# Combining expert outputs: a ring of nine slots in chunks of three tokens, one token of each chunk summed by TensorE

## The chip, the cores and the metric

The kernel runs on one core of one Trainium2 chip. The metric is the device time of one execution in microseconds; lower is better. The kernel before takes 707.68 us (median of three runs, 707.18 to 707.82). The profile is of one execution of 707.67 us; its span, in which the engines' records lie, is 705.5 us.

## The reference

```python
# expert_outputs: (16, 1024, 8, 512) float32; combine_weights: (16, 1024, 8) float32
def reference(expert_outputs, combine_weights):
    weights = combine_weights[..., np.newaxis]
    return np.sum(expert_outputs * weights, axis=2).astype(np.float32)
```

For each of 16,384 tokens, eight rows of 512 numbers are scaled by eight weights and added. A token brings in 16 KB and gives out 2 KB; all in all 268.4 MB of expert outputs and 0.5 MB of weights are read and 33.6 MB are written. Each number that is read is used in one multiplication and one addition.

## The kernel before

The tokens are spread over the 128 partitions, so a "token" below means one token of each partition: 128 token positions in all, each of them 2.097 MB of input and 0.262 MB of output. 120 of them go through a loop (`LOOP`), the last 8 through a tail (`TAIL`).

**The ring.** `ring` holds R = 10 tokens. A round fills it in three chunks of 4, 4 and 2 tokens (`CHUNKS`, L101), each one DMA with its own semaphore `loaded[c]`. There are 12 rounds. Each partition reads runs that lie together in memory: one partition's stretch is M = 40 tokens (640 KB), so this is the distance between the rows of one DMA.

**The engines.** Each engine has its own program, written out in order, and they meet at semaphores only.

- SyncE (`loads_and_last_stores`) issues all loads. From the second round on, a chunk's load waits until VectorE has finished the tokens that lay in those slots (L99, semaphore `done`, which counts finished tokens). After the loop it issues eight loads of one token each for the tail (L111), then the last round's store and the tail's stores in four pieces (L115).
- ScalarE (`weights_and_stores`) copies each round's weights from `w_t` into `w_c` (L136, two halves in turn) and issues the stores of the other rounds from `acc` (L91), each once its ten tokens are done. After the loop it makes the diagonal matrices for TensorE (L143): `ident` times one weight, 128x128, with five buffers in turn.
- VectorE (`terms`) does all sums of the loop. Per chunk one product of the first expert's rows by a broadcast weight (L189), then seven fused multiply-and-adds per token (L179), two tokens in turn. In the tail it adds the experts that TensorE leaves over.
- TensorE (`first_terms`) works in the tail alone. A product of a diagonal matrix of one weight and the 128x512 rows of one expert scales these rows; several of them accumulate in PSUM (`ps`). `pe_e` says how many experts of each tail token go this way: 43 products in all (L155).
- GpSimd makes the identity matrix at the start.

In the tail the tokens come in one by one, TensorE works on each as it lands, VectorE finishes it, and the stores go out as tokens become ready, the last one for a single token.

Of the kernel before, what the change touches and what calls it, by code (L numbers as in the profile page):

```python
# [10 lines left out]
def kernel(  # L11
# [17 lines left out]

    nc = tc.nc  # L30
    fp32 = mybir.dt.float32
    mult, add = mybir.AluOpType.mult, mybir.AluOpType.add

    B, S, E, D = expert_outputs.shape
    T = B * S
    P = 128
    R = 10
    G = 2 * R
    M = 2 * G
    T_P = T // P  # L40
    GROUPS = T_P // G
    LOOP = GROUPS * G
    TAIL = T_P - LOOP
    ROUNDS = LOOP // R
    CHUNKS = [(0, 4), (4, 4), (8, 2)]
    C = len(CHUNKS)
    DIAGS = 5

    x = expert_outputs.rearrange("b s e d -> (b s) e d")
    w = combine_weights.rearrange("b s e -> (b s) e")  # L50
    o = out.rearrange("b s d -> (b s) d")
    cut = LOOP * P
    x_g = x[0:cut].rearrange("(n p b g) e d -> n b p g e d", p=P, b=2, g=G)
    w_g = w[0:cut].rearrange("(n p m) e -> p n m e", p=P, m=M)
    o_g = o[0:cut].rearrange("(n p b g) d -> n b p g d", p=P, b=2, g=G)
    x_t = x[cut:T].rearrange("(p j) e d -> p j e d", j=TAIL)
    w_x = w[cut:T].rearrange("(p j) e -> p j e", j=TAIL)
    o_t = o[cut:T].rearrange("(p j) d -> p j d", j=TAIL)


    pe_e = [6, 6, 6, 6, 5, 5, 5, 4]
    tail_stores = [(0, 4), (4, 2), (6, 1), (7, 1)]
    diags = [(j, e) for j in range(TAIL) for e in range(pe_e[j])]
# [4 lines left out]
    acc = one.tile([P, G, D], fp32, name="acc")  # L68
    w_t = one.tile([P, T_P, E], fp32, name="w_t")
    w_c = one.tile([P, G, E], fp32, name="w_c")  # L70
    ident = one.tile([P, P], fp32, name="ident")
    diag = one.tile([P, DIAGS, P], fp32, name="diag")
    ps = psum.tile([P, TAIL, D], fp32, name="ps")

    sem = tc.alloc_semaphore
    w_in = sem("w_in")
    w_set = [sem(f"w_set{h}") for h in range(2)]
    loaded = [sem(f"loaded{c}") for c in range(C)]
    stored = [sem(f"stored{h}") for h in range(2)]
    step = sem("step")  # L80
    done = sem("done")
    tail_in = [sem(f"tail_in{j}") for j in range(TAIL)]
    tail_out = sem("tail_out")
    id_set = sem("id_set")
    diag_set = sem("diag_set")
    product = sem("product")

    def store(queue, n):
        h = n % 2
        queue.wait_ge(done, (n + 1) * R)  # L90
        queue.dma_start(  # L91
            out=o_g[n // 4, n // 2 % 2, :, h * R : h * R + R], in_=acc[:, h * R : h * R + R]
        ).then_inc(stored[h], 16)

    def loads_and_last_stores(sync):
        for n in range(ROUNDS):
            for c, (r, m) in enumerate(CHUNKS):
                if n:
                    sync.wait_ge(done, (n - 1) * R + r + m)  # L99
                g = n % 2 * R + r  # L100
                sync.dma_start(  # L101
                    out=ring[:, r : r + m], in_=x_g[n // 4, n // 2 % 2, :, g : g + m]
                ).then_inc(loaded[c], 16)
                if n == 0 and c == 0:
                    sync.dma_start(
                        out=w_t[:, 0:LOOP].rearrange("p (n m) e -> p n m e", m=M), in_=w_g
                    ).then_inc(w_in, 16)
                    sync.dma_start(out=w_t[:, LOOP:T_P], in_=w_x).then_inc(w_in, 16)
        for j in range(TAIL):
            sync.wait_ge(done, LOOP - R + j + 1)  # L110
            sync.dma_start(out=ring[:, j], in_=x_t[:, j]).then_inc(tail_in[j], 16)  # L111
        store(sync, ROUNDS - 1)
        for j, m in tail_stores:
            sync.wait_ge(done, LOOP + j + m)
            sync.dma_start(out=o_t[:, j : j + m], in_=acc[:, j : j + m]).then_inc(tail_out, 16)  # L115
# [13 lines left out]
    def weights_and_stores(scalar):  # L129
        scalar.wait_ge(w_in, 32)  # L130
        for n in range(ROUNDS):
            h = n % 2
            if n >= 2:
                store(scalar, n - 2)
                scalar.wait_ge(stored[h], 16 * (n // 2))
            scalar.copy(  # L136
                out=w_c[:, h * R : h * R + R], in_=w_t[:, n * R : n * R + R]
            ).then_inc(w_set[h], 1)
        store(scalar, ROUNDS - 2)
        scalar.wait_ge(stored[0], 16 * ROUNDS // 2)  # L140
        scalar.wait_ge(id_set, 2)
        for k, (j, e) in enumerate(diags):
            i = scalar.mul(out=diag[:, k % DIAGS], in_=ident, mul=w_t[:, LOOP + j, e : e + 1])  # L143
            i.then_inc(diag_set, 1)
            if k >= DIAGS:
                i.wait_op(product, k - DIAGS + 1, "sem-ge")
        scalar.wait_ge(stored[1], 16 * ROUNDS // 2)
        scalar.wait_ge(tail_out, 16 * len(tail_stores))

    def first_terms(tensor):  # L150
        for k, (j, e) in enumerate(diags):
            if e == 0:
                tensor.wait_ge(tail_in[j], 16)
            tensor.wait_ge(diag_set, k + 1)
            tensor.matmul(  # L155
                ps[:, j],
                lhsT=diag[:, k % DIAGS],
                rhs=ring[:, j, e],
                start=e == 0,
                stop=e == pe_e[j] - 1,  # L160
            ).then_inc(product, 1)

    def terms(vector):
        def take(s, v):
            vector.wait_ge(s, v).then_inc(s, -v)  # L165

        last = {}

        def count(i, g, e):

            if e == E - 1:
                i.then_inc(done, 1)
            else:
                i.then_inc(step, 1)
                last["all"] = last.get("all", 0) + 1
                last[g] = last["all"]

        def fused(g, e, weight, before):
            return vector.scalar_tensor_tensor(  # L179
                out=acc[:, g], in0=ring[:, g % R, e], scalar=weight, in1=before, op0=mult, op1=add  # L180
            )

        with nc.Fori(0, GROUPS, engines=OrderedEngineSet([vector.engine])):
            for h in range(2):
                take(w_set[h], 1)
                for c, (r, m) in enumerate(CHUNKS):
                    take(loaded[c], 16)
                    q = h * R + r
                    i = vector.tensor_tensor(  # L189
                        out=acc[:, q : q + m],  # L190
                        in0=ring[:, r : r + m, 0],
                        in1=w_c[:, q : q + m, 0:1].to_broadcast([P, m, D]),
                        op=mult,
                    )
                    i.then_inc(step, 1)
                    last["all"] = last.get("all", 0) + 1
                    last.update((g, last["all"]) for g in range(q, q + m))
                    for g in range(q, q + m, 2):
                        for e in range(1, E):
                            for k in (g, g + 1):  # L200
                                i = fused(k, e, w_c[:, k, e : e + 1], acc[:, k])
                                i.wait_op(step, last[k], "sem-ge")
                                count(i, k, e)
            take(step, last["all"])

        last.clear()
        for q in ((0, 1), (2,), (3,), (4,), (5,), (6,)):
            for e in range(pe_e[q[0]], E):
                for j in q:
                    weight = w_t[:, LOOP + j, e : e + 1]  # L210
                    if e == pe_e[j]:
                        i = fused(j, e, weight, ps[:, j])
                        i.wait_op(product, sum(pe_e[: j + 1]), "sem-ge")
                    else:
                        i = fused(j, e, weight, acc[:, j])
                        i.wait_op(step, last[j], "sem-ge")
                    count(i, j, e)

        j = TAIL - 1
        for e in range(pe_e[j], E):  # L220
            weight = w_t[:, LOOP + j, e : e + 1]
            if e == pe_e[j]:
                i = vector.tensor_scalar_mul(out=acc[:, j], in0=ring[:, j, e], scalar1=weight)  # L223
                i.wait_op(tail_in[j], 16, "sem-ge")
            else:
                i = fused(j, e, weight, acc[:, j])
                i.wait_op(step, last[j], "sem-ge")
            count(i, j, -1)
        vector.wait_ge(step, last[j])  # L229
        i = vector.tensor_tensor(out=acc[:, j], in0=acc[:, j], in1=ps[:, j], op=add)  # L230
        i.wait_op(product, len(diags), "sem-ge")
        count(i, j, E - 1)

    with tc.tile_critical(no_gpsimd_drain=True):  # L234
        loads_and_last_stores(nc.sync)
        identity(nc.gpsimd)
        weights_and_stores(nc.scalar)
        first_terms(nc.tensor)
        terms(nc.vector)
# [30 lines left out]
```

## Time and profile before

| what | value |
|---|---|
| time, median of three runs | 707.68 us |
| span of the profiled execution | 705.5 us |
| VectorE busy | 642.8 us |
| fused multiply-add on VectorE in the loop (L179) | 840 of 745 ns each |
| first term of a chunk (L189), 128x2048 and 128x1024 | 2287 ns and 1218 ns |
| TensorE pass of a product (L155) | 86 of 613 ns each |
| diagonal on ScalarE (L143) | 43 of 400 ns each |
| stores issued by ScalarE, issue to landing | 26.7 us (median of 11) |
| bytes moved | 302.53 MB, 429 GB/s over the span |

How to read it: the page first gives each engine's busy time and its share of the span, then what the DMA queues moved and for how much of the time of the sixteen DMA engines. The groups list the costliest lines of the kernel with the mean time of one instruction and the idle time of the engine ahead of them, with its releaser. A second view gives the busy times, the DMA share and the rate for chosen stretches of the span; the chain of waits follows the end of the execution back to what released it; the timeline lists instructions in order of time. PE is TensorE's product, PEld its loading of the stationary matrix, DVE is VectorE, ACT ScalarE, POOL GpSimd and SP SyncE.

### The profile page before, as it was taken

To read this page: it belongs to the slowest core of one execution; us is meant where nothing else is said; L and a number is where in the kernel's file an instruction comes from. 1 tells how busy PE (TensorE), PEld (TensorE's weight loads), DVE (VectorE), ACT (ScalarE), POOL (GpSimd) and SP (SyncE) were. 2 spreads that over 40 slices of the span, in tenths; PEclk is the share of its full clock that TensorE was granted. 3 is DMA by queue.
4 is the path that set the end of the run, shared out by engine and by line. 5 is a ranking of instruction groups with operands and counts; after the bars stand their busy time and mean duration, and the time that the engine had idled before them with its cause. 6 is when DMAs were issued, how large, how long until landed. Compare 5 with 4: busy or idle time off the path is not lost. (4 is left out here: it accounts for less than half of the span.)

```text
span 705.5 us, 1328 instructions
## 1 busy us (share of the span) xinstructions
PE 38.7 (5%) x86; PEld 16.9 (2%) x86; DVE 642.8 (91%) x898; ACT 21.1 (3%) x56; POOL 0.7 (0%) x6
## 2 busy tenths in 40 slices
PE   0000000000000000000000000000000000000695
PEld 0000000000000000000000000000000000000242
DVE  0599999979999989989999998998998998998964
ACT  0000000000000000000000000000000000000241
POOL 0000000000000000000000000000000000000000
PEclk9999999999999999999999999999999999999999
DMA  9999999999999999999999999999999999999997
GB/s 412 390 472 420 394 435 446 450 412 461 403 444 446 445 404 429 435 428 475 430 401 447 416 432 434 472 394 468 416 441 421 420 440 463 431 426 407 430 428 334
DMA packets 9186, 302.53 MB, mean 429 GB/s; under 512 B 1120, under 2 KB 1504, under 8 KB 1888
## 3 DMA queue, kind: packets, MB, share of 16 engines
q1 hardware_dynamic: 7600, 273.68, 90.0%
q10 hardware_dynamic: 1584, 28.84, 9.5%
q14 instruction: 2, 0.02, 0.0%
HBM read 268.96 MB, written 33.55 MB: 429 GB/s over the span
## 5 line engine op out<-in xcount | busy, mean ns | idle before, releaser
L179 DVE SCALAR_TENSOR_TENSOR acc<-ring,w_c,acc 128x512 f32<-128x512 f32 x840 | 559.7, 745 | 1.3
L189 DVE TENSOR_TENSOR acc<-ring,w_c 128x2048 f32<-128x2048 f32 (+1 forms) x36 | 69.5, 1931 | 46.2 <-DVEq L165 46.2
L155 PE MATMUL ps<-ring,diag 128*128 128x512 f32 x86 | 38.7, 613 | 659.1 <-DMA ring<-in_expert_outputs_dram 659.1
L155 PEld LDWEIGHTS ps<-ring,diag 128*128 128x128 f32 x86 | 16.9, 198 | 680.1 <-DMA ring<-in_expert_outputs_dram 659.1
L136 ACT COPY w_c<-w_t 128x80 f32<-128x80 f32 x12 | 3.0, 258 | 587.5 <-DMA out_dram<-acc 565.3
L143 ACT ACTIVATE diag<-ident,w_t 128x128 f32<-128x128 f32 x43 | 16.8, 400 | 84.4 <-DMA out_dram<-acc 54.2
L179 DVE SCALAR_TENSOR_TENSOR acc<-ring,w_t,ps 128x512 f32<-128x512 f32 x7 | 5.1, 744 | 9.6 <-PE ps L155 9.6
L179 DVE SCALAR_TENSOR_TENSOR acc<-ring,w_t,acc 128x512 f32<-128x512 f32 x13 | 9.7, 751 | 0.4
L136 ACT ACT_TABLE_LOAD x1 | 1.3, 1283 | 0.9 <-SPq L234 0.9
L230 DVE TENSOR_TENSOR acc<-acc,ps 128x512 f32<-128x512 f32 x1 | 0.7, 689 | 0.1
L223 DVE TENSOR_SCALAR acc<-ring,w_t 128x512 f32<-128x512 f32 x1 | 0.5, 481 | 0.0
L119 POOL TENSOR_SCALAR_AFFINE_SELECT ident<-ident 128x128 f32<-128x128 f32 x1 | 0.3, 292 | 0.1
L118 POOL MEMSET ident<- 128x128 f32 x1 | 0.2, 204 | 0.5 <-SPq L234 0.5
L254 POOL MEMSET const-bfloat16-1.0<- 128x1 bf16 x1 | 0.1, 101 | 0.0
L254 POOL MEMSET const-uint8-127<- 128x1 uint8 x1 | 0.1, 101 | 0.0
L254 POOL MEMSET const-float32-0.0<- 128x1 f32 x1 | 0.1, 98 | 0.2 <-issue 0.2
L254 POOL MEMSET const-float32-1.0<- 128x1 f32 x1 | 0.1, 98 | 0.0
## 6 DMA issues: line engine op xcount, KB each, us to landing
ring<-in_expert_outputs_dram SPq DMA_DIRECT2D x12, 4096.0 KB, 34.0
out_dram<-acc ACTq DMA_DIRECT2D x11, 2560.0 KB, 26.7
ring<-in_expert_outputs_dram SPq DMA_DIRECT2D x8, 2048.0 KB, 28.6
out_dram<-acc SPq DMA_DIRECT2D x1, 2560.0 KB, 24.8
out_dram<-acc SPq DMA_DIRECT2D x1, 1024.0 KB, 17.7
out_dram<-acc SPq DMA_DIRECT2D x1, 512.0 KB, 9.0
out_dram<-acc SPq DMA_DIRECT2D x2, 256.0 KB, 4.7
w_t<-in_combine_weights_dram SPq DMA_DIRECT2D x1, 480.0 KB, 22.6
```

The lines of the kernel that those rows point to most:

```text
L118: gpsimd.memset(ident, 0.0).then_inc(id_set, 1)
L119: gpsimd.affine_select(out=ident, in_=ident, compare_op=mybir.AluOpType.not_equal, fill=1.0, base=0, pattern=[[-1, P]], channel_multiplier ...
L136: scalar.copy(out=w_c[:, h * R : h * R + R], in_=w_t[:, n * R : n * R + R]).then_inc(w_set[h], 1)
L143: i = scalar.mul(out=diag[:, k % DIAGS], in_=ident, mul=w_t[:, LOOP + j, e : e + 1])
L155: tensor.matmul(ps[:, j], lhsT=diag[:, k % DIAGS], rhs=ring[:, j, e], start=e == 0, stop=e == pe_e[j] - 1,).then_inc(product, 1)
L179: return vector.scalar_tensor_tensor(out=acc[:, g], in0=ring[:, g % R, e], scalar=weight, in1=before, op0=mult, op1=add)
L189: i = vector.tensor_tensor(out=acc[:, q : q + m], in0=ring[:, r : r + m, 0], in1=w_c[:, q : q + m, 0:1].to_broadcast([P, m, D]), op=mult,)
L223: i = vector.tensor_scalar_mul(out=acc[:, j], in0=ring[:, j, e], scalar1=weight)
L230: i = vector.tensor_tensor(out=acc[:, j], in0=acc[:, j], in1=ps[:, j], op=add)
L254: nc = _bacc.Bacc("TRN2", target_bir_lowering=False, num_devices=1)
```

## The change

The change moves a third of the loop's sums from VectorE to TensorE, and cuts all work into equal pieces.

- The ring has nine slots in three chunks of three tokens. With M = 63 tokens a partition, 126 tokens go through the loop in 14 rounds, and the tail has two tokens.
- Of each chunk, VectorE sums the first two tokens as before. For the third it makes eight diagonal matrices with one instruction (`ident` broadcast over experts, times the weights broadcast over columns) and raises `fed`; TensorE, in a loop of its own, forms eight products that accumulate in one bank of PSUM, and ScalarE copies the sum into `acc`.
- A chunk is done when its semaphore `summed[c]` has three counts, two from VectorE and one from ScalarE. Loads and stores wait for it in place of `done`.
- ScalarE no longer makes diagonals. Its copies from PSUM, the weights' copies and the stores stand in one order; a wait for the store of the round before now stands between the second and the third copy of a round.
- SyncE issues the two loads of the tail once the last round's first chunk is done, then the stores of the last two rounds (`HELD`), then one store for both tail tokens.
- In the tail, VectorE makes eight diagonals (four experts of each token) with one instruction, TensorE sums four experts of each token, and VectorE adds the other four.

```diff
-    R = 10
+    R = 9
+    C = 3
+    V = C - 1
     G = 2 * R
-    M = 2 * G
+    M = 7 * R
...
-    CHUNKS = [(0, 4), (4, 4), (8, 2)]
-    C = len(CHUNKS)
-    DIAGS = 5
+    CHUNKS = R // C
+    HELD = 2
+    K = 4
...
     def loads_and_last_stores(sync):
...
-                    sync.wait_ge(done, (n - 1) * R + r + m)
+                    sync.wait_ge(summed[c], n * C)
...
+        sync.wait_ge(summed[0], ROUNDS * C)
         for j in range(TAIL):
-            sync.wait_ge(done, LOOP - R + j + 1)
             sync.dma_start(out=ring[:, j], in_=x_t[:, j]).then_inc(tail_in[j], 16)
-        store(sync, ROUNDS - 1)
-        for j, m in tail_stores:
-            sync.wait_ge(done, LOOP + j + m)
-            sync.dma_start(out=o_t[:, j : j + m], in_=acc[:, j : j + m]).then_inc(tail_out, 16)
+        for n in range(ROUNDS - HELD, ROUNDS):
+            store(sync, n)
+        sync.wait_ge(done, TAIL)
+        sync.dma_start(out=o_t, in_=acc_t).then_inc(tail_out, 16)
...
+        for n in range(ROUNDS):
+            for c in range(CHUNKS):
+                i = scalar.copy(out=acc[:, n % 2 * R + c * C + V], in_=ps[:, c])
+                i.wait_op(product, (n * CHUNKS + c + 1) * E, "sem-ge").then_inc(summed[c], 1)
+                if c == 1 and 1 <= n < ROUNDS - 1:
+                    scalar.wait_ge(stored[(n - 1) % 2], 16 * ((n - 1) // 2 + 1))
+                    weights(n + 1)
+            if n < ROUNDS - HELD:
+                store(scalar, n)
...
+        with nc.Fori(0, ROUNDS, engines=this):
+            for c in range(CHUNKS):
+                take(tensor, fed, 1)
+                products(ps[:, c], diag[:, c], c * C + V, E)
+        tensor.wait_ge(fed, 1)
+        for j in range(TAIL):
+            tensor.wait_ge(tail_in[j], 16)
+            products(ps_t[:, j], diag_t[:, j], j, K)
...
+                for c in range(CHUNKS):
+                    take(vector, loaded[c], 16)
+                    s = c * C
+                    g = h * R + s
+                    vector.tensor_tensor(
+                        out=diag[:, c],
+                        in0=ident[:, None, :].to_broadcast([P, E, P]),
+                        in1=w_c[:, g + V, :, None].to_broadcast([P, E, P]),
                         op=mult,
-                    )
-                    i.then_inc(step, 1)
+                    ).then_inc(fed, 1)
+                    vector.tensor_tensor(
+                        out=acc[:, g : g + V],
+                        in0=ring[:, s : s + V, 0],
+                        in1=w_c[:, g : g + V, 0:1].to_broadcast([P, V, D]),
+                        op=mult,
+                    ).then_inc(step, 1)
...
+                    for e in range(1, E):
+                        for k in range(V):
+                            weight = w_c[:, g + k, e : e + 1]
+                            i = fused(acc[:, g + k], ring[:, s + k, e], weight, acc[:, g + k])
+                            i.wait_op(step, last[k], "sem-ge")
+                            count(i, k, e, summed[c])
...
+        vector.tensor_tensor(
+            out=diag_t,
+            in0=ident[:, None, None, :].to_broadcast([P, TAIL, K, P]),
+            in1=w_t[:, LOOP:T_P, 0:K, None].to_broadcast([P, TAIL, K, P]),
+            op=mult,
+        ).then_inc(fed, 1)
+        for e in range(K, E):
+            for j in range(TAIL):
+                weight = w_t[:, LOOP + j, e : e + 1]
+                if e == K:
+                    i = fused(acc_t[:, j], ring[:, j, e], weight, ps_t[:, j])
+                    i.wait_op(product, ROUNDS * CHUNKS * E + K * (j + 1), "sem-ge")
+                else:
+                    i = fused(acc_t[:, j], ring[:, j, e], weight, acc_t[:, j])
+                    i.wait_op(step, last[j], "sem-ge")
+                count(i, j, e, done)
```

More of the change, by code (lines that the diff above doesn't have):

```diff
@@ L36 @@
     P = 128
-    R = 10
+    R = 9
+    C = 3
+    V = C - 1
     G = 2 * R
-    M = 2 * G
+    M = 7 * R
     T_P = T // P
-    GROUPS = T_P // G
-    LOOP = GROUPS * G
+    LOOP = T_P // M * M
     TAIL = T_P - LOOP
     ROUNDS = LOOP // R
-    CHUNKS = [(0, 4), (4, 4), (8, 2)]
-    C = len(CHUNKS)
-    DIAGS = 5
+    CHUNKS = R // C
+    HELD = 2
+    K = 4
+    assert TAIL <= C and ROUNDS % 2 == 0
     x = expert_outputs.rearrange("b s e d -> (b s) e d")
@@ L52 @@
     cut = LOOP * P
-    x_g = x[0:cut].rearrange("(n p b g) e d -> n b p g e d", p=P, b=2, g=G)
-    w_g = w[0:cut].rearrange("(n p m) e -> p n m e", p=P, m=M)
-    o_g = o[0:cut].rearrange("(n p b g) d -> n b p g d", p=P, b=2, g=G)
+    x_m = x[0:cut].rearrange("(n p k r) e d -> n k p r e d", p=P, k=M // R, r=R)
+    w_m = w[0:cut].rearrange("(n p m) e -> p n m e", p=P, m=M)
+    o_m = o[0:cut].rearrange("(n p k r) d -> n k p r d", p=P, k=M // R, r=R)
     x_t = x[cut:T].rearrange("(p j) e d -> p j e d", j=TAIL)
@@ L58 @@
     o_t = o[cut:T].rearrange("(p j) d -> p j d", j=TAIL)
-    pe_e = [6, 6, 6, 6, 5, 5, 5, 4]
-    tail_stores = [(0, 4), (4, 2), (6, 1), (7, 1)]
-    diags = [(j, e) for j in range(TAIL) for e in range(pe_e[j])]
     one = ctx.enter_context(tc.tile_pool(name="one", bufs=1))
@@ L68 @@
     acc = one.tile([P, G, D], fp32, name="acc")
+    acc_t = one.tile([P, TAIL, D], fp32, name="acc_t")
     w_t = one.tile([P, T_P, E], fp32, name="w_t")
@@ L71 @@
     ident = one.tile([P, P], fp32, name="ident")
-    diag = one.tile([P, DIAGS, P], fp32, name="diag")
-    ps = psum.tile([P, TAIL, D], fp32, name="ps")
+    diag = one.tile([P, CHUNKS, E, P], fp32, name="diag")
+    diag_t = one.tile([P, TAIL, K, P], fp32, name="diag_t")
+    ps = psum.tile([P, CHUNKS, D], fp32, name="ps")
+    ps_t = psum.tile([P, TAIL, D], fp32, name="ps_t")
     sem = tc.alloc_semaphore
@@ L77 @@
     w_set = [sem(f"w_set{h}") for h in range(2)]
-    loaded = [sem(f"loaded{c}") for c in range(C)]
+    loaded = [sem(f"loaded{c}") for c in range(CHUNKS)]
     stored = [sem(f"stored{h}") for h in range(2)]
@@ L81 @@
     done = sem("done")
+    fed = sem("fed")
+    product = sem("product")
+    summed = [sem(f"summed{c}") for c in range(CHUNKS)]
     tail_in = [sem(f"tail_in{j}") for j in range(TAIL)]
@@ L84 @@
     id_set = sem("id_set")
-    diag_set = sem("diag_set")
-    product = sem("product")
     def store(queue, n):
         h = n % 2
-        queue.wait_ge(done, (n + 1) * R)
+        queue.wait_ge(summed[-1], (n + 1) * C)
         queue.dma_start(
-            out=o_g[n // 4, n // 2 % 2, :, h * R : h * R + R], in_=acc[:, h * R : h * R + R]
+            out=o_m[n * R // M, n % (M // R)], in_=acc[:, h * R : h * R + R]
         ).then_inc(stored[h], 16)
@@ L96, in loads_and_last_stores @@
         for n in range(ROUNDS):
-            for c, (r, m) in enumerate(CHUNKS):
+            for c in range(CHUNKS):
                 if n:
-                    sync.wait_ge(done, (n - 1) * R + r + m)
-                g = n % 2 * R + r
+                    sync.wait_ge(summed[c], n * C)
                 sync.dma_start(
-                    out=ring[:, r : r + m], in_=x_g[n // 4, n // 2 % 2, :, g : g + m]
+                    out=ring[:, c * C : c * C + C],
+                    in_=x_m[n * R // M, n % (M // R), :, c * C : c * C + C],
                 ).then_inc(loaded[c], 16)
@@ L105, in loads_and_last_stores @@
                     sync.dma_start(
-                        out=w_t[:, 0:LOOP].rearrange("p (n m) e -> p n m e", m=M), in_=w_g
+                        out=w_t[:, 0:LOOP].rearrange("p (n m) e -> p n m e", m=M), in_=w_m
                     ).then_inc(w_in, 16)
                     sync.dma_start(out=w_t[:, LOOP:T_P], in_=w_x).then_inc(w_in, 16)
+        sync.wait_ge(summed[0], ROUNDS * C)
         for j in range(TAIL):
-            sync.wait_ge(done, LOOP - R + j + 1)
             sync.dma_start(out=ring[:, j], in_=x_t[:, j]).then_inc(tail_in[j], 16)
-        store(sync, ROUNDS - 1)
-        for j, m in tail_stores:
-            sync.wait_ge(done, LOOP + j + m)
-            sync.dma_start(out=o_t[:, j : j + m], in_=acc[:, j : j + m]).then_inc(tail_out, 16)
+        for n in range(ROUNDS - HELD, ROUNDS):
+            store(sync, n)
+        sync.wait_ge(done, TAIL)
+        sync.dma_start(out=o_t, in_=acc_t).then_inc(tail_out, 16)
     def identity(gpsimd):
@@ L127, in identity, with weights_sums_and_stores, weights @@
         ).wait_op(id_set, 1, "sem-ge").then_inc(id_set, 1)
-    def weights_and_stores(scalar):
-        scalar.wait_ge(w_in, 32)
-        for n in range(ROUNDS):
+    def weights_sums_and_stores(scalar):
+        def weights(n):
             h = n % 2
-            if n >= 2:
-                store(scalar, n - 2)
-                scalar.wait_ge(stored[h], 16 * (n // 2))
             scalar.copy(
@@ L138, in weights_and_stores @@
             ).then_inc(w_set[h], 1)
-        store(scalar, ROUNDS - 2)
-        scalar.wait_ge(stored[0], 16 * ROUNDS // 2)
         scalar.wait_ge(id_set, 2)
[L142 to L161, printed above, removed]
+        scalar.wait_ge(w_in, 32)
+        weights(0)
+        weights(1)
@@ new lines, in weights_sums_and_stores @@
+        for n in range(ROUNDS):
[7 more added lines that the diff above has]
+                store(scalar, n)
+        for h in range(2):
+            scalar.wait_ge(stored[h], 16 * ROUNDS // 2)
@@ new lines, in weights_sums_and_stores, with take, last_tokens, products @@
+        scalar.wait_ge(tail_out, 16)
+    def take(engine, s, v):
+        engine.wait_ge(s, v).then_inc(s, -v)
+    def last_tokens(tensor):
+        def products(out, left_of, j, terms):
+            for e in range(terms):
+                tensor.matmul(
+                    out, lhsT=left_of[:, e], rhs=ring[:, j, e], start=e == 0, stop=e == terms - 1
+                ).then_inc(product, 1)
+        this = OrderedEngineSet([tensor.engine])
+        with nc.Fori(0, ROUNDS, engines=this):
[6 more added lines that the diff above has]
+            products(ps_t[:, j], diag_t[:, j], j, K)
@@ L163, in terms, with count @@
     def terms(vector):
-        def take(s, v):
-            vector.wait_ge(s, v).then_inc(s, -v)
         last = {}
-        def count(i, g, e):
+        def count(i, g, e, end):
             if e == E - 1:
-                i.then_inc(done, 1)
+                i.then_inc(end, 1)
             else:
@@ L176, in count, with fused @@
                 last[g] = last["all"]
-        def fused(g, e, weight, before):
+        def fused(out, x, weight, before):
             return vector.scalar_tensor_tensor(
-                out=acc[:, g], in0=ring[:, g % R, e], scalar=weight, in1=before, op0=mult, op1=add
+                out=out, in0=x, scalar=weight, in1=before, op0=mult, op1=add
             )
-        with nc.Fori(0, GROUPS, engines=OrderedEngineSet([vector.engine])):
+        this = OrderedEngineSet([vector.engine])
+        with nc.Fori(0, ROUNDS // 2, engines=this):
@@ L184, in terms @@
             for h in range(2):
[L185 to L192, printed above, removed]
-                        op=mult,
-                    )
-                    i.then_inc(step, 1)
-                    last["all"] = last.get("all", 0) + 1
[L197 to L203, printed above, removed]
@@ L204, in terms @@
-            take(step, last["all"])
-        last.clear()
[L207 to L230, printed above, removed]
@@ L231, in terms @@
-        i.wait_op(product, len(diags), "sem-ge")
-        count(i, j, E - 1)
+                take(vector, w_set[h], 1)
+                for c in range(CHUNKS):
+                    take(vector, loaded[c], 16)
[5 more added lines that the diff above has]
+                        in1=w_c[:, g + V, :, None].to_broadcast([P, E, P]),
+                        op=mult,
+                    ).then_inc(fed, 1)
[5 more added lines that the diff above has]
+                    ).then_inc(step, 1)
+                    last["all"] = last.get("all", 0) + 1
+                    last.update((k, last["all"]) for k in range(V))
+                    for e in range(1, E):
[4 more added lines that the diff above has]
+                            count(i, k, e, summed[c])
@@ new lines, in terms @@
+            take(vector, step, last["all"])
+        last.clear()
+        vector.tensor_tensor(
[14 more added lines that the diff above has]
+                count(i, j, e, done)
@@ L236 @@
         identity(nc.gpsimd)
-        weights_and_stores(nc.scalar)
-        first_terms(nc.tensor)
+        weights_sums_and_stores(nc.scalar)
+        last_tokens(nc.tensor)
         terms(nc.vector)
```

## The prediction

> **What bounds the kernel now.** I read the page first (engine shares, then the DMA queues), then a table of windows, the chain of waits and the timeline of the end.
>
> ```profile
> span 705.5 us, 1328 instructions
> PE 38.7 (5%) x86; PEld 16.9 (2%) x86; DVE 642.8 (91%) x898; ACT 21.1 (3%) x56; POOL 0.7 (0%) x6
> q1 hardware_dynamic: 7600, 273.68, 90.0%
> q10 hardware_dynamic: 1584, 28.84, 9.5%
> ```
>
> VectorE at 91% tempts. But the two DMA queues together keep the sixteen engines busy 90.0 + 9.5 = 99.5% of the span. The windows (length; busy us of PE, PEld, DVE, ACT, POOL with counts; clock, DMA share, GB/s) say when:
>
> ```profile
> 20.00:640.00 620.00, 0.00 (x0) 0.00 (x0) 594.70 (x831) 3.00 (x12) 0.00 (x0) 1.00 1.00 432
> 692.00:700.00 8.00, 5.83 (x14) 2.28 (x12) 5.74 (x9) 1.07 (x3) 0.00 (x0) 1.00 0.99 420
> 700.00:705.50 5.50, 0.00 (x0) 0.00 (x0) 0.32 (x1) 0.00 (x0) 0.00 (x0) 0.79 0.37 145
> ```
>
> DMA share is 1.00 at 432 GB/s through the loop and 0.99 until 700 us. Only the last 5.5 us are not full. 302.53 MB at 432 GB/s is 700.3 us, which with the launch and the last store is the span. So the **DMA engines** are the bound, and VectorE is merely close to them: a chunk of four tokens brings 8.39 MB in and 1.05 MB out, 9.44 / 432 = 21.9 us, against 21.0 us on VectorE, which the timeline shows:
>
> ```profile
> 643.09 2.29 DVE L189 TENSOR_TENSOR acc<-ring,w_c 128x2048 f32<-128x2048 f32 x1 [2.06 <-DVEq L165]
> 645.42 18.64 DVE L179 SCALAR_TENSOR_TENSOR acc<-ring,w_c,acc 128x512 f32<-128x512 f32 x28
> 663.97 1.22 DVE L189 TENSOR_TENSOR acc<-ring,w_c 128x1024 f32<-128x1024 f32 x1
> 699.63 0.69 DVE L230 TENSOR_TENSOR acc<-acc,ps 128x512 f32<-128x512 f32 x1
> ```
>
> 28 fused operations in 18.64 us are one each 0.666 us (a single one lasts 745 ns, but they overlap). VectorE waited 2.06 us for that chunk's load. The last VectorE operation ends at 700.32, and 5.2 us later the span ends: a 256 KB store and its acknowledgment. The chain gives an anchor for landings:
>
> ```profile
> 631.12 27.93 DMA ring<-in_expert_outputs_dram
> 659.09 35.33 PE ps L155 x78
> ```
>
> The first load of the tail landed at 659.05. By then 121 token loads (2.097 MB each), 110 token stores (0.262 MB each) and the weights (0.52 MB) had passed: 283.1 MB. At 432 GB/s they take 655.4 us. A landing is thus bytes / 432 plus 3.65 us.
>
> TensorE, from the timeline and the groups:
>
> ```profile
> 660.11 0.34 PEld L155 LDWEIGHTS ps<-ring,diag 128*128 128x128 f32 x1 [0.52 <-issue]
> 660.96 0.34 PEld L155 LDWEIGHTS ps<-ring,diag 128*128 128x128 f32 x1 [0.52 <-issue]
> 663.34 0.19 PEld L155 LDWEIGHTS ps<-ring,diag 128*128 128x128 f32 x1 [0.24 <-issue]
> 663.77 0.19 PEld L155 LDWEIGHTS ps<-ring,diag 128*128 128x128 f32 x1 [0.24 <-issue]
> L155 PE MATMUL ps<-ring,diag 128*128 128x512 f32 x86 | 38.7, 613 | 659.1 <-DMA ring<-in_expert_outputs_dram 659.1
> ```
>
> 86 records for 43 products: two passes each. A pass takes 0.85 us for the first 3.4 us of work, then 0.43 us.
>
> [...] The pitch of x goes from 40 to 63 tokens of 16 KB (640 to 1008 KB)[...]; the trace shows only the first, at full rate. [...]
>
> **The change, part by part.**
>
> 1. *VectorE in the loop.* A chunk of three tokens costs one 128x1024 product for the diagonals (1.22 us, the row of that size above; broadcast operands, same element count), one 128x1024 first term (1.22) and 14 fused operations (9.4): 11.9 us with gaps. 42 chunks are 500 us. The DMA needs 6.29 + 0.79 = 7.08 MB, 16.4 us a chunk. VectorE now idles 4.5 us a chunk, and that **gains nothing**: the DMA was full before.
>
> 2. *Ring.* Three chunks of three slots. A chunk is free 12 us after it lands and is wanted again when the two others have been moved, 33 us after: 20 us of slack, so the DMA queue stays filled. Cost nothing.
>
> 3. *TensorE in the loop.* Eight products, sixteen passes, starting cold: 4 x 0.85 + 12 x 0.43 = 8.6 us, done 10 us after the chunk's start, inside VectorE's 11.9. [...] Its wait for the diagonals holds only its own products.
>
> 4. *ScalarE.* One copy from PSUM per chunk. No such row before: 0.40 us (its 128x128 activation) [...]: hidden, as TensorE ends 1.9 us before VectorE. The new wait for the store of the round before stands ahead of the next weights and the round's last copy, behind which a load and a store wait; that store was issued two chunk times (33 us) earlier and stores took 26.7 us to land: hidden.
>
> 5. *Bytes.* Same 302.5 MB. Loads of 48 KB a row in place of 64 and 32, stores of 18 KB in place of 20: no change taken.
>
> 6. *The end.* Here it costs. The last loop chunk lands when all but two token loads, two stores of nine tokens and the tail store have passed: 126 loads (264.2 MB), 108 token stores (28.3), weights: 293.1 MB, 10.0 MB after the anchor, so at 659.05 + 23.1 = **682.1**. Behind it lie only 4.2 MB of tail loads (landed by 692) and 4.7 MB of held stores (11 us more, to about 703). Beside them runs a serial chain of computation: VectorE's chunk 11.9 to 694.1; the tail's diagonals, which VectorE makes only then, 1.2, to 695.4; eight products of TensorE, 6.9 warm, to 702.4; from the second token's sum on, seven fused operations, 6 x 0.666 + 0.745 = 4.7, to 707.2; the last store, 5.2 as before plus 0.6 for twice the bytes (half a MB against a quarter, at 432), to **713.0**. Before, ScalarE had made the first diagonals ahead, 40 us of products ran beside loads, and stores went out in four pieces, so that the DMA was full until its last quarter MB. Is TensorE warm there? Its last chunk ends 10.0 us after 682.1, the tail begins at 13.3: 3.3 us idle[...]. I take warm; cold adds 4 x 0.42 = 1.7.
>
> 7. *The start.* First load 6.3 MB, VectorE begins some 5 us earlier: worth nothing.
>
> Sum: the span goes from 705.5 to 713.0; time minus span was 707.67 - 705.5 = 2.2, so **715.2 us**, 7.5 slower. The 7.5 is 6.9 more between the last VectorE operation (700.3 to 707.2) and 0.6 of store.
>
> **The rivals.**
>
> - *Same chain, TensorE cold at the end*: 716.9.
> - *The DMA runs at its ceiling.* [...] Against: 432 already holds over 620 us.
> - *VectorE was what held the loads back*, [...] and the end is hidden as well as before. For: VectorE's 91%, and SyncE waiting nearly always on VectorE before issuing. [...] Against: share 1.00, so SyncE's waits ended before the queue ran dry; and the chain above is too long to hide behind 11 us of stores.
> - *The end is hidden, the rate unchanged*: 707.7, no difference.
> - *The loop slows*, by the new pitch [...] or by TensorE and VectorE reading beside DMA writes. 2% of 678 us is 13.6: 729. The trace shows no sign, and can't for a pitch it hasn't.
>
> **How the numbers follow.** Likeliest 0.50 (715.2); cold 0.24 (716.9); ceiling 0.11 [...]; faster 0.05; no difference 0.03; slow loop 0.07. The range 710.0 to 718.0 holds the first three, 0.85, with 1 us for the sum of small gaps. Faster 0.05, same 0.03, slower 0.92.
>
> **What would show it.** Right: a DMA share near 1.00 at about 432 GB/s up to 690 us, then windows at a half or less between 703 and 709; VectorE busy near 510 us with an idle of 4 to 5 us a chunk, put down to loads; a chain that runs at its end through VectorE's last chunk, the tail's diagonals, TensorE and seven fused operations. Wrong: a loop rate off 432 by more than 0.3%, chunks over 12.5 us on VectorE, products of the tail over 9 us, or the tail's diagonals made while loads are still landing.

## The result and the profile after

The changed kernel takes **712.16 us** (median of six runs) against 707.57 us of the kernel before: slower by 4.6 us, where 7.5 us were forecast; the time lies inside the range. The recorded ratio of the two kernels is 1.0073, with a 95% interval of 1.006 to 1.0086. One of the six executions took 1853.12 us, with TensorE passes of 3028 ns each in its profile, and is left out of that ratio. The profile read below is of another execution of the same kernel (`after_look`, 711.72 us).

The head of its page, the DMA queues, and the group of VectorE's first operation in each chunk:

```profile
span 709.9 us, 2389 instructions
PE 399.5 (56%) x688; PEld 163.1 (23%) x688; DVE 499.1 (70%) x681; ACT 28.1 (4%) x57; POOL 0.7 (0%) x6
q1 hardware_dynamic: 7184, 274.21, 89.6%
q10 hardware_dynamic: 1728, 28.31, 9.3%
L200 DVE TENSOR_TENSOR diag<-ident,w_c 128x1024 f32<-128x1024 f32 x42 | 51.4, 1225 | 199.0 <-DVEq L156 199.0
```

VectorE was relieved of 143.7 us (642.8 to 499.1) and the time grew. Of the 199.0 us of idle time ahead of a chunk's first operation, 22.0 lie ahead of the first chunk, until the first weights were copied; the others are waits for loads. The windows of the changed kernel (the same columns as before):

```profile
20.00:640.00 620.00, 356.12 (x610) 145.43 (x611) 447.91 (x610) 25.73 (x53) 0.00 (x0) 0.77 1.00 433
692.00:700.00 8.00, 6.36 (x16) 2.75 (x15) 2.83 (x4) 0.58 (x1) 0.00 (x0) 1.00 1.01 435
700.00:705.00 5.00, 1.28 (x3) 0.21 (x2) 3.69 (x6) 0.00 (x0) 0.00 (x0) 1.00 0.08 33
705.00:715.00 10.00, 0.00 (x0) 0.00 (x0) 1.03 (x2) 0.00 (x0) 0.00 (x0) 0.67 0.13 52
```

The loop moves 433 GB/s, where it moved 432 (experiment 1 shows that this is no difference). From 700 to 705 us the DMA engines are busy 8% of the time, while VectorE still computes. The chain that ended last, in order of time (start, length, what):

```profile
681.19 1.22 DVE diag L200
682.41 1.15 DVE acc L206
683.56 0.03 issue
683.59 8.11 DVE acc L188 x13
...
692.95 1.15 DVE diag_t L223
694.10 0.04 issue
694.14 7.15 PE ps_t L161 x16
701.29 0.02 issue
701.31 4.72 DVE acc_t L188 x7
```

No transfer is in it: from the moment the last loop chunk is in, at 681 us, one computation waits for the next until 706.03 us.

### The profile page after: what moved, and what is told of

It reads as the page before. It is cut to its first block, busy times and chain, and to the rows that moved or that the text cites. A ratio compares the mean times of both kernels' runs of the same rounds, so it can differ in the third digit from the quotient of the medians.

```text
span 1851.4 us, 2389 instructions
## 1 busy us (share of the span) xinstructions
PE 1819.2 (98%) x688; PEld 636.7 (34%) x688; DVE 499.1 (27%) x681; ACT 28.1 (2%) x57; POOL 0.7 (0%) x6
## 4 chain that ended last, share of the span: by engine, by line
PE 98%; DVE 0%; issue 0%
PE ps L161 96%; PE ps_t L161 2%; DVE acc_t L188 0%
## 5 line engine op out<-in xcount | busy, mean ns | idle before, releaser
L161 PE MATMUL ps<-ring,diag 128*128 128x512 f32 x672 | 1776.9, 3028 | 23.5 <-PEq L156 23.5
L161 PEld LDWEIGHTS ps<-ring,diag 128*128 128x128 f32 x672 | 621.7, 926 | 1173.9 <-issue 1173.9
L188 DVE SCALAR_TENSOR_TENSOR acc<-ring,w_c,acc 128x512 f32<-128x512 f32 x588 | 393.3, 747 | 1.5
L200 DVE TENSOR_TENSOR diag<-ident,w_c 128x1024 f32<-128x1024 f32 x42 | 51.5, 1226 | 1209.3 <-DVEq L156 1209.3
L206 DVE TENSOR_TENSOR acc<-ring,w_c 128x1024 f32<-128x1024 f32 x42 | 51.2, 1218 | 0.0
L144 ACT COPY acc<-ps 128x512 f32<-128x512 f32 x42 | 24.6, 585 | 1752.6 <-PE ps L161 1752.6
L161 PE MATMUL ps_t<-ring,diag_t 128*128 128x512 f32 x16 | 42.7, 3054 | 0.0
L161 PEld LDWEIGHTS ps_t<-ring,diag_t 128*128 128x128 f32 x16 | 15.0, 935 | 27.4 <-issue 27.4
L188 DVE SCALAR_TENSOR_TENSOR acc_t<-ring,w_t,acc_t 128x512 f32<-128x512 f32 x6 | 4.1, 746 | 0.0
```

The source lines that it names most:

```text
L144: i = scalar.copy(out=acc[:, n % 2 * R + c * C + V], in_=ps[:, c])
L161: tensor.matmul(out, lhsT=left_of[:, e], rhs=ring[:, j, e], start=e == 0, stop=e == terms - 1).then_inc(product, 1)
L188: return vector.scalar_tensor_tensor(out=out, in0=x, scalar=weight, in1=before, op0=mult, op1=add)
L200: vector.tensor_tensor(out=diag[:, c], in0=ident[:, None, :].to_broadcast([P, E, P]), in1=w_c[:, g + V, :, None].to_broadcast([P, E, P]), ...
L206: vector.tensor_tensor(out=acc[:, g : g + V], in0=ring[:, s : s + V, 0], in1=w_c[:, g : g + V, 0:1].to_broadcast([P, V, D]), op=mult,).the ...
```

## The experiments

**1. The changed kernel again**, unedited, for its trace.

> The changed kernel as it is. My theory: the loop is bound by the DMA engines at the same 432 GB/s as before, and the whole loss is the serial chain after the last loop chunk; 712 us, with the last chunk landing near 682 us and some 12 us on VectorE for it. Rival: the loop's rate rose above 432 GB/s (which would account for the 3 us by which the kernel is faster than I forecast) and the end is as long as forecast; then the last chunk lands near 679 us.

712.11 us (median). VectorE starts on the last chunk at 681.19, nearer to the 682 of the one theory than to the 679 of the other. The step from 432 to 433 GB/s hangs on where the window is cut: from 22 to 642 us both kernels show 433. Counted from the start of the span, the kernel before and the changed one have moved the same:

```profile
0.00:640.00 640.00, 0.00 (x0) 0.00 (x0) 594.70 (x831) 4.28 (x13) 0.70 (x6) 1.00 1.00 431
```
```profile
0.00:640.00 640.00, 356.12 (x610) 145.43 (x611) 447.91 (x610) 25.73 (x53) 0.70 (x6) 0.78 1.00 431
```

So the rival falls: the loop did not become faster. Why the last chunk was in 0.9 us before the forecast stays open. The larger part of the surplus, 1.9 us, lies behind VectorE's last operation (see below).

**2. The tail's diagonals made ahead of the loop.**

```diff
+        vector.wait_ge(id_set, 2)
+        vector.wait_ge(w_in, 32)
+        vector.tensor_tensor(out=diag_t, ...).then_inc(fed_t, 1)
         this = OrderedEngineSet([vector.engine])
         with nc.Fori(0, ROUNDS // 2, engines=this):
...
-        tensor.wait_ge(fed, 1)
+        tensor.wait_ge(fed_t, 1)
```

> The tail's eight diagonals are made ahead of the loop. My theory, the serial chain: TensorE starts the tail right after its last chunk and VectorE makes one product less, so the end comes 3.3 us earlier, 708.8 us. Rival, the end waits for the held stores on the DMA queue and not for the computation: 712 us, no change.

709.62 us (ratio to the kernel before 1.0028, 1.0018 to 1.0038): 2.5 us earlier by the medians, 2.1 us by the two profiled executions. The end does wait for this chain. That it was not 3.3 is TensorE's doing. Its timeline in the changed kernel (a bracket is the idle time ahead of the first pass), then the chain with early diagonals:

```profile
36.10 8.80 PE L161 MATMUL ps<-ring,diag 128*128 128x512 f32 x16 [2.57 <-PEq L156]
...
668.04 8.67 PE L161 MATMUL ps<-ring,diag 128*128 128x512 f32 x16 [5.42 <-PEq L156]
682.56 9.94 PE L161 MATMUL ps<-ring,diag 128*128 128x512 f32 x16 [5.85 <-PEq L156]
694.14 7.13 PE L161 MATMUL ps_t<-ring,diag_t 128*128 128x512 f32 x16 [1.64 <-DVE diag_t L223]
```

```profile
682.88 9.44 PE ps L162 x16
692.32 6.88 PE ps_t L162 x16
699.23 4.72 DVE acc_t L189 x7
```

The last chunk's sixteen passes took 9.9 us, not the 8.6 that I had worked out, so TensorE had stood idle for 1.64 us only. The tail now starts 1.8 us earlier (692.32 for 694.14) and its passes take 0.3 us less (6.88 for 7.15): the 2.1 us of the traces. No more could be won by starting it sooner.

**3. VectorE sums all three tokens of a chunk.** TensorE and ScalarE's copies from PSUM leave the loop; the weights' copies move to the head of each round.

```diff
-    V = C - 1
+    V = C
...
-                i = scalar.copy(out=acc[:, n % 2 * R + c * C + V], in_=ps[:, c])
-                i.wait_op(product, (n * CHUNKS + c + 1) * E, "sem-ge").then_inc(summed[c], 1)
...
-        with nc.Fori(0, ROUNDS, engines=this):
-            for c in range(CHUNKS):
-                take(tensor, fed, 1)
-                products(ps[:, c], diag[:, c], c * C + V, E)
...
-                    vector.tensor_tensor(out=diag[:, c], ...).then_inc(fed, 1)
```

> VectorE sums all three tokens of each chunk (15.8 us a chunk against 16.4 us of DMA); TensorE works in the tail alone. My theory: the loop moves at the same rate and the last chunk takes 3.9 us longer, with TensorE cold in the tail up to 1.7 more: 716 to 718 us. Rival, unloading VectorE is what raised the loop's rate: the loop loses that too, 720 us or more.

721.29 us, ratio 1.0189 (1.0175 to 1.0203): above the range of the theory. The number fits the rival, but its reason does not hold, as the loop's rate is untouched:

```profile
20.00:640.00 620.00, 0.00 (x0) 0.00 (x0) 598.87 (x837) 4.70 (x15) 0.00 (x0) 1.00 1.00 433
```

What I had overlooked shows in VectorE's timeline, its last five chunks (two of them left out):

```profile
622.63 1.76 DVE L192 TENSOR_TENSOR acc<-ring,w_c 128x1536 f32<-128x1536 f32 x1 [1.67 <-DVEq L153]
638.47 1.76 DVE L192 TENSOR_TENSOR acc<-ring,w_c 128x1536 f32<-128x1536 f32 x1
...
685.59 1.75 DVE L192 TENSOR_TENSOR acc<-ring,w_c 128x1536 f32<-128x1536 f32 x1
```

The chunks follow each other at 15.7 us without a wait. The last stores are held back, so a chunk of loads alone passes in 6.29 MB / 433 = 14.5 us, the distance at which VectorE started its last chunks in the changed kernel (666.67, 681.19); VectorE falls behind and starts on the last chunk at 685.59, 4.4 us later than in the changed kernel. The longer chunk (3.9) and a TensorE that is cold in the tail, having stood idle through the loop (8.6 us against 7.15, 1.4), are the terms that were forecast; together 9.7 of the 9.9 us between the spans (719.8 and 709.9). So the offload is worth 9.2 us to **this** tiling, all of it after the last stores are held back; while loads and stores run together it is worth nothing.

**4. The tail's sums left out**, but for the first term of each token: no diagonals, no TensorE, two operations on VectorE. Loads and stores all stay.

```diff
-        vector.tensor_tensor(out=diag_t, ...).then_inc(fed, 1)
-        for e in range(K, E):
...
+        for j in range(TAIL):
+            i = vector.tensor_scalar_mul(
+                out=acc_t[:, j], in0=ring[:, j, 0], scalar1=w_t[:, LOOP + j, 0:1])
+            i.wait_op(tail_in[j], 16, "sem-ge")
+            i.then_inc(done, 1)
```

> Leaves out the sums of the two tail tokens but for the first term (no diagonals, no TensorE, two VectorE operations); all loads and stores stay. My theory: the end is then set by the held stores, 705 to 708 us, as before the change. Rival, the end is bound by the DMA queue anyway: 712 us.

706.43 us, ratio 0.9981 (0.9974 to 0.9989). The tail's computation beyond that first term costs 5.7 us of exposed time, more than the whole loss. What is left is set by the DMA queue: the tail's store was issued at 694.18, and landed 9.2 us later, behind the held stores.

```profile
out_dram<-acc_t SPq DMA_DIRECT2D x1, 512.0 KB, 9.2
```

**5. Fewer experts of the tail for TensorE.** `K = 4` becomes `K = 2`.

> TensorE takes two experts of each tail token in place of four, VectorE six. My theory, the serial chain, counts 4 products less at 0.86 us (3.4 us earlier) and four fused operations more at 0.666 us after the last product (2.7 us later), and the diagonals of half the size 0.5 us less: 710.9 us. Rival, the sums of the tail aren't the path and the held stores are: 712.1 us.

710.78 us, within 0.1 us of the chain's sum. Where the work of the tail is done matters little, since both engines stand in the same chain.

**6. Two stores in the tail** instead of one.

```diff
-        sync.wait_ge(done, TAIL)
-        sync.dma_start(out=o_t, in_=acc_t).then_inc(tail_out, 16)
+        for j in range(TAIL):
+            sync.wait_ge(done, j + 1)
+            sync.dma_start(out=o_t[:, j : j + 1], in_=acc_t[:, j : j + 1]).then_inc(tail_out, 16)
```

> The changed kernel with one store per tail token in place of one for both. In the changed kernel the 512 KB store landed 2.6 us after its issue, on an idle queue; before, the last 256 KB store took at least 3.9 us behind others. If the queue ahead set that difference, the second store of a pair waits little: 711.5 to 712.1 us. Rival, each store of such a pair costs 3.9 us or more: 713.4 us.

711.48 us, against the rival. The DMA issues of the kernels before, after and with two stores (engine, operation, count, size, median us to landing):

```profile
out_dram<-acc SPq DMA_DIRECT2D x2, 256.0 KB, 4.7
```
```profile
out_dram<-acc_t SPq DMA_DIRECT2D x1, 512.0 KB, 2.6
```
```profile
out_dram<-acc_t SPq DMA_DIRECT2D x2, 256.0 KB, 2.0
```

The same 256 KB take 4.7 us (3.9 at the least) at the end of the kernel before, behind other stores, and 2.0 us on a queue that has run empty.

**7. The chain taken apart.** Early diagonals, and VectorE sums its four experts of each tail token while TensorE works, adding the sums from PSUM last.

```diff
         for e in range(K, E):
             for j in range(TAIL):
...
                 if e == K:
-                    i = fused(acc_t[:, j], ring[:, j, e], weight, ps_t[:, j])
-                    i.wait_op(product, ROUNDS * CHUNKS * E + K * (j + 1), "sem-ge")
+                    i = vector.tensor_scalar_mul(out=acc_t[:, j], in0=ring[:, j, e], scalar1=weight)
+                    i.wait_op(tail_in[j], 16, "sem-ge")
...
+        for j in range(TAIL):
+            vector.wait_ge(step, last[j])
+            i = vector.tensor_tensor(out=acc_t[:, j], in0=acc_t[:, j], in1=ps_t[:, j], op=add)
+            i.wait_op(product, ROUNDS * CHUNKS * E + K * (j + 1), "sem-ge")
```

> The tail's diagonals are made ahead of the loop, and VectorE sums its four experts of each tail token while TensorE works, adding TensorE's sums last. My theory, the serial chain: VectorE's last operation ends near 700 us, before the held stores have passed, so the time is that of the kernel without the tail's sums, 706.4 us (up to 707.0). Rival, the products of TensorE set the end whatever VectorE does: 709.6 us, as with the early diagonals alone.

**706.44 us**, ratio 0.9984 (0.9977 to 0.999): all of the loss is recovered, and the kernel is 1.1 us faster than the one before. VectorE's timeline and the window that was empty:

```profile
693.31 0.88 DVE L236 TENSOR_SCALAR acc_t<-ring,w_t 128x512 f32<-128x512 f32 x2
694.11 4.06 DVE L189 SCALAR_TENSOR_TENSOR acc_t<-ring,w_t,acc_t 128x512 f32<-128x512 f32 x6
698.08 0.68 DVE L246 TENSOR_TENSOR acc_t<-acc_t,ps_t 128x512 f32<-128x512 f32 x1
699.92 0.69 DVE L246 TENSOR_TENSOR acc_t<-acc_t,ps_t 128x512 f32<-128x512 f32 x1 [1.16 <-PE ps_t L162]
```
```profile
700.00:705.00 5.00, 0.00 (x0) 0.00 (x0) 0.61 (x1) 0.00 (x0) 0.00 (x0) 0.75 0.38 156
```

VectorE ends at 700.6, 5.4 us earlier than in the changed kernel, while the held stores are still passing (the last one landed at 702.2), and the time is that of the kernel without the tail's sums. The two limits now meet: the tail's store, issued at 700.63, landed 2.8 us later, hardly more than the 2.6 of an idle queue, and at the same 703.4 as in experiment 4, where it had waited behind the held stores. By these figures a longer tail would show at once.

**8. The same with two stores.**

> Early diagonals, VectorE's terms ahead of TensorE's sums, and one store per tail token. My theory: the DMA queue's held stores set the end, and the first token's store goes out 3 us earlier behind them: 706.4 us, no better than with one store. Rival, the last store's own latency is what is left after the queue has drained: 705.8 us or less.

706.46 us: no better. The two stores took 3.8 and 2.7 us to land, not the 2.0 of an idle queue; the first landed just behind the held ones.

## Why the prediction was right or wrong

*The bound.* Right: 1.00 of the DMA engines at 432 to 433 GB/s in the loop, with VectorE busy for 91%, 70% and (experiment 3) 93% of the span. The rivals in which relieving VectorE pays in the loop fall, and so do those in which the loop runs faster than 432 GB/s (a ceiling above that was my supposition, which no trace had shown) or slows: at the new pitch it moved as much as before, 431 GB/s from 0 to 640 us in both kernels. *The start* was worth nothing, as forecast, but VectorE began 2.9 us earlier (22.04 for 24.90) and not 5, since it waited for the weights.

*The loop's parts.* VectorE's chunk was 11.8 us (681.19 to 692.96), forecast 11.9; the copy from PSUM 585 ns (128x512; the 128x128 activation of before took 400); idle time 4.3 us ahead of each of the 41 chunks after the first, forecast 4.5. TensorE's chunk of 8.6 us was too small: the products of the 42 chunks kept it busy for 392.4 us, 9.3 a chunk, and the last chunk took 9.94. So it did not end 1.9 us before VectorE: of the last chunk ScalarE's copy was done at 693.12, VectorE's sums at 692.96, and 11 of the 39 loads that wait for slots were released by ScalarE. That cost nothing in the loop, and showed only in experiment 2.

*The end*, term by term, as forecast and as measured:

| term | forecast | measured |
|---|---|---|
| VectorE starts on the last chunk | 682.1 | 681.19 |
| its chunk done, tail's diagonals done | 694.1, 695.4 | 692.96, 694.1 |
| TensorE's tail | 6.9 | 7.15 |
| seven fused operations | 4.7 | 4.72 |
| VectorE's last operation ends | 707.2 | 706.03 |
| from there to the end of the span | 5.8 | 3.9 |

The chain is right in every link; experiments 2, 5 and 7 moved it through the links they touched. Of the 3.1 us by which the span was forecast too long, 0.9 come with the earlier landing and 0.4 from a shorter chunk and diagonals, TensorE's tail takes 0.2 back, and 1.9 lie behind VectorE's last operation. **The mis-sized term is the last store**: "the last store, 5.2 as before plus 0.6 for twice the bytes". Of the 5.2 us, 3.9 were the landing of a store that stood behind others, and 1.3 lay between the landing and the end of the span. I used them for a store that, by the same forecast, would find the queue empty. It did (the last held store had landed at 701.8), and landed in 2.6 us, not 3.9 + 0.6 = 4.5; the 1.3 us stayed.

*TensorE warm in the tail.* Right in the profiled execution, with passes of 592 ns but for one of 697 ns, but by luck. The forecast took 3.3 us of idle time to be short enough, which no trace had shown; in this trace TensorE was slow again after 2.57 us (the second chunk, 8.80 us, in experiment 2). The tail found it idle for 1.64 us only, as the chunk's passes took longer than forecast, and took 7.15 us. Three of the eleven executions of the changed kernel near 712 us took 713.65 to 714.09; that is about what a cold tail would add (1.7 by the forecast, 1.4 in experiment 3), but none of them has a trace, so this is not shown.

## What to carry to other kernels

When the DMA engines are full, as here (a share of 1.00 at 432 to 433 GB/s), don't expect taking work off a compute engine to pay in the loop (143.7 us less on VectorE left the rate as it was); ask what runs after the last loads have landed, and count that chain link by link. Let the transfers that are left at the end take longer than the computation that is left, and let each engine do its independent share of the tail ahead of the sum that joins them (here 5.7 us, more than the change had lost). Take a duration for a transfer from a row with the same queue ahead of it, busy or empty (for 256 KB here 3.9 us or more against 2.0).

## What the runs showed of the hardware

A 256 KB store landed 2.0 us after its issue on an idle queue and 3.9 us or more behind other stores; for 512 KB it was 2.6 us on an idle queue and 9.2 us behind the held stores. TensorE, idle for 2.57, 5.42 or 10.26 us ahead of a chunk, was back at slower passes (1195 ns at the longest, against 592), and the sixteen passes took 8.80, 8.67 and 9.96 us, against 6.9 us where they followed on at once and 7.15 after 1.64 us (experiment 2). And rows of 48 KB at a pitch of 1008 KB moved at the same rate, within 0.3%, as rows of 64 and 32 KB at 640 KB (431 GB/s from 0 to 640 us).
